# Silu activations and high-part splits of gated values held back until the next unit by seven has issued its copies out of PSUM

## The chip, the core and the metric

The kernel runs on one core of a Trainium2 chip. TensorE (PE) multiplies matrices and sums into PSUM; VectorE (DVE) and ScalarE (ACT) do elementwise work and read PSUM; GpSimd (POOL) helps in some stages; SyncE (SP) issues most DMAs. Each engine works through its own queue in a fixed order, and waits on semaphores for the others. The metric is the device time of one execution in microseconds: 1941.19 us before, the median of three runs between 1939.77 and 1942.38.

## What is computed

A decoder trunk of two layers over 512 tokens of width 1024, in float32. Each layer is: half a feed-forward block, a mixer (an mLSTM in the first layer, sparse attention in the second), half a feed-forward block. The change lies in the feed-forward block:

```python
def swiglu(h, w_in, w_out):
    a, b = jnp.split(h @ w_in, 2, axis=-1)
    return (jax.nn.silu(a) * b) @ w_out

h = h + 0.5 * swiglu(rmsnorm(h, ffn_norm[layer, 0]), ffn_w_in[layer, 0], ffn_w_out[layer, 0])
```

There are four such blocks, with 1024 inputs, 2 x 2816 columns of `w_in` (`a` and `b`) and 2816 rows of `w_out`.

## The kernel before

All of it stays on the core: eight tiles `h` of 128 features x 512 tokens hold the stream. The stages follow each other as `ffn0`, `mlstm`, `ffn1`, `kv`, `ffn2`, `nsa`, `ffn3`. To keep float32 accuracy every operand of a matmul is split in two: ScalarE copies it rounded into a high part (`whi`, `xhi`, `ghi`, L245 or L167), VectorE subtracts that from the value for the low part (`wlo`, `xlo`, `glo`, L246 or L170), and TensorE makes three products of parts (`mm3`, L236).

Columns of `w_in` are taken in blocks of 128, 22 for `a` and 22 for `b`. In the blocks 0, 1 and 3 (`SEVEN`) most pairs of blocks are multiplied as 2 x 2 block matrices by a scheme with seven products in place of eight: a **unit by seven** (`by_seven`, L473). Its seven products of 12 matmuls each go into three PSUM tiles A, Z, B of 512 columns, each half for itself: (1) A left, (2) Z right, (3) B left, (4) A right, (5) Z left, (6) Z right, (7) A left. Products 1, 5 and 6 take the normed input (`xhi`, `xlo`), products 2, 3, 4 and 7 sums of its quarters (`thi`, `tlo`). After each of the first four products ScalarE copies a half tile to SBUF (L481): `fw` after 1, `fu` after 2 and 3, `fw` after 4. Product 5 adds onto Z, where product 2 has been copied from, so it waits for the second copy. VectorE then adds Z (L497) and A (L502), and the unit returns two blocks of columns, `u1` and `u2`.

Gate blocks and value blocks alternate: a unit on two blocks of `a`, then a unit on the two blocks of `b` that go with them. After the gate unit `silu` (L403) multiplies by the norm's factor (L406, VectorE) and activates (L408, ScalarE). After the value unit `gate` (L411) multiplies both (L415, VectorE; L414 first in the last third) and splits the product into `ghi` and `glo`. The 22 pairs of blocks are taken in thirds of 8, 8 and 6 (`EVENS`); after each third the parts of its gated values are multiplied by the rows of `w_out` (the down product, weights `wraw`, splits at L167 and L170).

The weights of a unit are fetched as four quarters `q` (256 KB each), VectorE makes four sums of them (L197 to L200, `s`), and the seven forms are split in four groups, one unit ahead of TensorE. A scheduler below the program decides each engine's order within what the code's sequence and the data allow; `with tc.issue_after(ins)` holds instructions of the block behind `ins` on its own engine. The splits of the next unit's weights, the four copies, the activations and the `ghi` splits all share ScalarE's queue.

## Time and profile before

| what | value |
|---|---|
| median of three runs | 1941.19 us |
| profiled execution, its own time | 1940.4 us |
| its span, first to last instruction | 1938.6 us |
| granted TensorE clock, mean | 0.998 |
| PE / DVE / ACT busy | 99% / 81% / 53% of the span |
| copies of units (L481) | 57 units x 4 copies |
| activations behind units and strips (L408) | 66, 631 ns each |
| `ghi` splits (L245) | 88, 628 ns each |

[...] Matmuls of 256 columns last 0.28 us and start every 0.11 us. In the time line a bracket at the end of a row gives how long the engine sat idle before it and what ended that. A row of windows gives the stretch, its length, then busy time and count for each engine shown, the granted clock, the DMA share and GB/s.

### The profile page before, as it was taken

To read this page: it belongs to the slowest core of one execution; us is meant where nothing else is said; L and a number is where in the kernel's file an instruction comes from. 1 tells how busy PE (TensorE), PEld (TensorE's weight loads), DVE (VectorE), ACT (ScalarE), POOL (GpSimd) and SP (SyncE) were. 2 spreads that over 40 slices of the span, in tenths; PEclk is the share of its full clock that TensorE was granted. 3 is DMA by queue.
4 is the path that set the end of the run, shared out by engine and by line. 5 is a ranking of instruction groups with operands and counts; after the bars stand their busy time and mean duration, and the time that the engine had idled before them with its cause. 6 is when DMAs were issued, how large, how long until landed. Compare 5 with 4: busy or idle time off the path is not lost. (4 is left out here: it accounts for less than half of the span.)

```text
span 1938.6 us, 31636 instructions
## 1 busy us (share of the span) xinstructions
PE 1913.0 (99%) x11946; PEld 1693.3 (87%) x11946; DVE 1567.4 (81%) x2947; ACT 1024.9 (53%) x1979; POOL 168.1 (9%) x222
## 2 busy tenths in 40 slices
PE   9999999999999999999999999999999999999999
PEld 7989898788878999898888989898877788999897
DVE  8969788757889879697676979696899989879695
ACT  6536345445656446265354535354777766445262
POOL 0000001012200000001100000001444410000000
PEclk9999999999999999999999999999999999999999
DMA  5333322323132323323343332323322222323322
GB/s 192 115 98 104 120 83 71 116 82 96 66 126 82 122 86 104 103 72 116 117 129 107 115 113 101 103 66 113 107 66 55 66 100 86 120 88 105 101 74 93
DMA packets 81945, 192.80 MB, mean 99 GB/s; under 512 B 9920, under 2 KB 10944, under 8 KB 81792
## 3 DMA queue, kind: packets, MB, share of 16 engines
q1 hardware_dynamic: 80272, 187.76, 30.3%
q8 instruction: 94, 1.54, 0.3%
q0 software_dynamic: 512, 1.31, 0.3%
q10 hardware_dynamic: 1008, 1.70, 0.2%
q14 instruction: 59, 0.48, 0.1%
HBM read 177.10 MB, written 2.10 MB: 92 GB/s over the span
## 5 line engine op out<-in xcount | busy, mean ns | idle before, releaser
L236 PE MATMUL pmm<-xhi,whi 128*128 128x256 f32 (+1 forms) x1376 | 441.4, 321 | 6.7 <-ACT fu L481 6.1
L236 PE MATMUL pmm<-xhi,wlo 128*128 128x256 f32 (+1 forms) x1376 | 437.5, 318 | 0.4 <-DVE wlo L170 0.4
L236 PE MATMUL pmm<-xlo,whi 128*128 128x256 f32 (+1 forms) x1376 | 437.0, 318 | 0.8 <-DVE xlo L290 0.8
L167 ACT ACTIVATE whi<-wraw 128x512 fp32r<-128x512 f32 (+3 forms) x258 | 204.8, 810 | 269.6 <-PE pmm L236 163.2
L236 PE MATMUL pmm<-thi,whi 128*128 128x256 f32 x1184 | 328.8, 278 | 2.4 <-ACT fw L516 2.0
L236 PE MATMUL pmm<-thi,wlo 128*128 128x256 f32 x1184 | 327.5, 277 | 1.4 <-DVE wlo L246 1.4
L236 PE MATMUL pmm<-tlo,whi 128*128 128x256 f32 x1184 | 327.7, 277 | 0.0
L170 DVE TENSOR_TENSOR wlo<-wraw,whi 128x512 fp32r<-128x512 f32 (+3 forms) x258 | 240.3, 944 | 70.6 <-ACT whi L167 67.8
L236 PEld LDWEIGHTS pmm<-xhi,whi 128*128 128x128 f32 x1376 | 258.4, 188 | 26.2 <-ACT fu L481 7.7
L236 PEld LDWEIGHTS pmm<-xhi,wlo 128*128 128x128 f32 x1376 | 258.4, 188 | 20.1 <-DVE wlo L170 0.7
L236 PEld LDWEIGHTS pmm<-xlo,whi 128*128 128x128 f32 x1376 | 258.6, 188 | 19.8 <-DVE xlo L290 2.6
L245 ACT ACTIVATE whi<-q 128x512 fp32r<-128x512 f32 x260 | 163.9, 631 | 209.1 <-PE pmm L236 156.1
L236 PE MATMUL pmm<-glo,whi 128*128 128x512 f32 x704 | 274.4, 390 | 0.0
L236 PE MATMUL pmm<-ghi,whi 128*128 128x512 f32 x704 | 274.2, 389 | 0.0
L236 PE MATMUL pmm<-ghi,wlo 128*128 128x512 f32 x704 | 273.9, 389 | 0.0
L236 PEld LDWEIGHTS pmm<-thi,whi 128*128 128x128 f32 x1184 | 223.2, 189 | 4.0 <-ACT fw L516 3.3
L236 PEld LDWEIGHTS pmm<-thi,wlo 128*128 128x128 f32 x1184 | 223.0, 188 | 1.6 <-DVE wlo L246 1.6
L236 PEld LDWEIGHTS pmm<-tlo,whi 128*128 128x128 f32 x1184 | 223.4, 189 | 0.0
L246 DVE TENSOR_TENSOR wlo<-q,whi 128x512 fp32r<-128x512 f32 x260 | 178.0, 685 | 16.4 <-ACT whi L245 16.4
L245 ACT ACTIVATE whi<-s 128x512 fp32r<-128x512 f32 x222 | 138.5, 624 | 54.6 <-PE pmm L236 32.7
L236 PEld LDWEIGHTS pmm<-glo,whi 128*128 128x128 f32 x704 | 132.2, 188 | 28.0 <-DVE glo L246 1.1
L236 PEld LDWEIGHTS pmm<-ghi,wlo 128*128 128x128 f32 x704 | 132.2, 188 | 27.6
(380 smaller groups left out, 3246.7 us busy)
## 6 DMA issues: line engine op xcount, KB each, us to landing
q<-in_ffn_in SPq DMA_DIRECT2D x260, 256.0 KB, 2.6
wraw<-in_ffn_out SPq DMA_DIRECT2D x48, 512.0 KB, 3.5
wraw<-in_ffn_out SPq DMA_DIRECT2D x48, 384.0 KB, 3.1
wraw<-in_ffn_in SPq DMA_DIRECT2D x27, 512.0 KB, 3.8
e<-in_ffn_in SPq DMA_DIRECT2D x36, 256.0 KB, 2.7
wraw<-in_m_qk SPq DMA_DIRECT2D x8, 512.0 KB, 3.6
wraw<-in_m_v SPq DMA_DIRECT2D x8, 512.0 KB, 3.6
wraw<-in_m_og SPq DMA_DIRECT2D x8, 512.0 KB, 3.6
```

The lines of the kernel that those rows point to most:

```text
L167: t = nc.scalar.activation(hi[:p, c], raw[:p, c], AF.Copy)
L170: nc.vector.tensor_tensor(lo[:p, c], raw[:p, c], hi[:p, c].bitcast(F32), op=ALU.subtract)
L236: self.nc.tensor.matmul(out, lhsT, rhs, start=start, stop=stop, skip_group_check=shared)
L245: self.nc.scalar.activation(hi, src, AF.Copy)
L246: self.nc.vector.tensor_tensor(lo, src, hi.bitcast(F32), op=ALU.subtract)
```

## The change

Two closures are kept in a list `parked` in the three layers with units by seven: the activation of a gate value (L408; its multiplication at L406 is still issued at once), and the allocation and split of a gated value into `ghi` and `glo` (the multiplications are still issued at once). The next unit by seven issues what is kept directly after the copy of A right, the last of its four copies, and holds the ScalarE part of it behind that copy. At the end of each third, before the down product, what is still kept is issued. Gated values of the two plain blocks at a layer's start are not kept.

```diff
+            parked = deque()
+
+            def unpark():
+                while parked:
+                    parked.popleft()()
+
-            def silu(pa):
+            def silu(pa, park=False):
                 t = gp.tile([P, T], F32, name="ft", tag="ft", bufs=3 if seven else 2)
                 if seven:
                     TT(t, pa, r, op=ALU.mult)
                     pa = t
-                nc.scalar.activation(t, pa, AF.Silu)
+                if park:
+                    parked.append(lambda: nc.scalar.activation(t, t, AF.Silu))
+                else:
+                    nc.scalar.activation(t, pa, AF.Silu)
                 return t
...
                 TT(t, t, u, op=ALU.mult)
                 bufs = 8 if seven or not k0 else 6
-                hi = gp.tile([P, T], F32R, name="ghi", tag="ghi", bufs=bufs)
-                lo = gp.tile([P, T], F32R, name="glo", tag="glo", bufs=bufs)
-                self.split(t, hi, lo)
-                gs.append((hi, lo))
+
+                def parts():
+                    hi = gp.tile([P, T], F32R, name="ghi", tag="ghi", bufs=bufs)
+                    lo = gp.tile([P, T], F32R, name="glo", tag="glo", bufs=bufs)
+                    self.split(t, hi, lo)
+                    gs.append((hi, lo))
+
+                if park:
+                    parked.append(parts)
+                else:
+                    parts()
...
                 yield from product(A[:, l], s2, -2, False)
-                out(u1[:, r], A[:, l])
+                with tc.issue_after(out(u1[:, r], A[:, l]).ins):
+                    unpark()
...
-                            ts = [silu(t) for t in (yield from by_seven(p))]
+                            ts = [silu(t, seven) for t in (yield from by_seven(p))]
...
-                                ts.append(silu(pa))
+                                ts.append(silu(pa, seven))
                         for t, u in zip(ts, (yield from by_seven(FB + p))):
-                            gate(t, u)
+                            gate(t, u, seven)
...
+                unpark()
                 n = k1 - k0
                 for m in range(0, KB, 2):
```

The orders of TensorE, SyncE and GpSimd are the same before and after. Those of ScalarE and VectorE change in the three layers. The first place is ScalarE in the last layer, second third, in the gate unit with the blocks 14 and 15, where `ghi` belongs to the values of blocks 12 and 13. Before:

```order
L481 ACTIVATE fw_20059<-pmm_20056 128x256
L245 ACTIVATE ghi_20047<-ft_19908 128x512
L245 ACTIVATE whi_20106<-q11_19956 128x512
L245 ACTIVATE ghi_20052<-ft_19911 128x512
L481 ACTIVATE fu_20060<-pmm_20057 128x256
L245 ACTIVATE whi_20106<-s1_20091 128x512
L481 ACTIVATE fu_20060<-pmm_20058 128x256
L245 ACTIVATE whi_20138<-q22_19962 128x512
L481 ACTIVATE fw_20059<-pmm_20056 128x256
```

After (L497 is the copy's line there):

```order
L497 ACTIVATE fw_20051<-pmm_20048 128x256
L245 ACTIVATE whi_20098<-q11_19954 128x512
L497 ACTIVATE fu_20052<-pmm_20049 128x256
L245 ACTIVATE whi_20098<-s1_20083 128x512
L497 ACTIVATE fu_20052<-pmm_20050 128x256
L245 ACTIVATE whi_20138<-q22_19960 128x512
L497 ACTIVATE fw_20051<-pmm_20048 128x256
L245 ACTIVATE ghi_20130<-ft_19908 128x512
L245 ACTIVATE ghi_20134<-ft_19910 128x512
L245 ACTIVATE whi_20138<-s2_20084 128x512
```

The two `ghi` splits stood between the first and the second copy and now stand behind the fourth. The second place is VectorE in the same unit, from the gate's last multiplication on. Before:

```order
L415 TENSOR_TENSOR ft_19911<-ft_19911,fu_19918 128x512
L246 TENSOR_TENSOR wlo_20062<-q21_19822,whi_20061 128x512
L246 TENSOR_TENSOR glo_20048<-ft_19908,ghi_20047 128x512
L246 TENSOR_TENSOR glo_20053<-ft_19911,ghi_20052 128x512
L200 TENSOR_TENSOR s4_20093<-q12_19958,s2_20092 128x512
L246 TENSOR_TENSOR wlo_20107<-q11_19956,whi_20106 128x512
L246 TENSOR_TENSOR wlo_20107<-s1_20091,whi_20106 128x512
L246 TENSOR_TENSOR wlo_20139<-q22_19962,whi_20138 128x512
```

After (L424 is the multiplication's line):

```order
L424 TENSOR_TENSOR ft_19910<-ft_19910,fu_19916 128x512
L246 TENSOR_TENSOR wlo_20054<-q21_19814,whi_20053 128x512
L198 TENSOR_TENSOR s2_20084<-s1_20083,q11_19954 128x512
L246 TENSOR_TENSOR wlo_20099<-q11_19954,whi_20098 128x512
L200 TENSOR_TENSOR s4_20085<-q12_19956,s2_20084 128x512
L246 TENSOR_TENSOR wlo_20099<-s1_20083,whi_20098 128x512
L197 TENSOR_TENSOR s1_20227<-q21_20094,q22_20096 128x512
L246 TENSOR_TENSOR wlo_20139<-q22_19960,whi_20138 128x512
L199 TENSOR_TENSOR q21_20094<-q11_20090,q21_20094 128x512
L246 TENSOR_TENSOR glo_20131<-ft_19908,ghi_20130 128x512
L246 TENSOR_TENSOR glo_20135<-ft_19910,ghi_20134 128x512
```

The two `glo` subtractions came one operation behind the gate's multiplication and now come eight behind it; sums and low parts of the next units stand ahead of them. The third place is ScalarE in the value unit that ends this third. Before:

```order
L481 ACTIVATE fw_20197<-pmm_20194 128x256
L408 ACTIVATE ft_20188<-ft_20188 128x512
L408 ACTIVATE ft_20191<-ft_20191 128x512
L481 ACTIVATE fu_20198<-pmm_20195 128x256
L167 ACTIVATE whi_20238<-wraw_20236 128x1024
L481 ACTIVATE fu_20198<-pmm_20196 128x256
L481 ACTIVATE fw_20197<-pmm_20194 128x256
L167 ACTIVATE whi_20270<-wraw_20268 128x1024
```

After (L415 is the activation's line):

```order
L497 ACTIVATE fw_20195<-pmm_20192 128x256
L497 ACTIVATE fu_20196<-pmm_20193 128x256
L167 ACTIVATE whi_20236<-wraw_20234 128x1024
L497 ACTIVATE fu_20196<-pmm_20194 128x256
L497 ACTIVATE fw_20195<-pmm_20192 128x256
L415 ACTIVATE ft_20188<-ft_20188 128x512
L415 ACTIVATE ft_20190<-ft_20190 128x512
L167 ACTIVATE whi_20270<-wraw_20268 128x1024
```

The two activations moved from behind the first copy to behind the fourth, ahead of the split of the down product's second weight.

## The prediction

> **What bounds the kernel now.** I read the page first, then the list of waits, then the chain that ended last, and then the time line around the longest stall.

> ```profile
> span 1938.6 us, 31636 instructions
> PE 1913.0 (99%) x11946; PEld 1693.3 (87%) x11946; DVE 1567.4 (81%) x2947; ACT 1024.9 (53%) x1979; POOL 168.1 (9%) x222
> ```

> TensorE (PE) is busy for 1913.0 of 1938.6 us, so 25.6 us of idle time is nearly all that a change of order can win. The list of waits says who causes it (microseconds in total, times, longest):

> ```profile
> PE pmm L236 <- ACT fu L481: 6.1, 7, 2.0
> PE pmm L236 <- ACT fw L516: 2.0, 4, 0.7
> ```

> The first row is the largest single cause: seven times a matmul waits for a copy of a sum out of PSUM (`fu`, L481) on ScalarE (ACT). These copies belong to the units by seven. The second row is the other form of unit, which the change doesn't touch. The chain that ended last shows why such a copy is late:

> ```profile
> 1886.13 0.61 DVE ft L415
> ...
> 1886.77 0.97 ACT ghi L245 x2
> ...
> 1887.91 0.38 ACT fu L481
> ```

> VectorE (DVE) makes a gated value (L415), ScalarE waits for it to split off its high part (`ghi`), and the copy stands behind that split in ScalarE's queue. The longest stall, on ScalarE, VectorE and TensorE:

> ```profile
> 1779.11 0.38 ACT L481 ACTIVATE fw<-pmm 128x256 f32<-128x256 f32 x1 [0.79 <-PE pmm L236]
> 1783.16 0.63 ACT L245 ACTIVATE ghi<-ft 128x512 fp32r<-128x512 f32 x1 [3.66 <-DVE ft L415]
> 1783.69 0.61 ACT L245 ACTIVATE whi<-q 128x512 fp32r<-128x512 f32 x1
> 1784.21 0.61 ACT L245 ACTIVATE ghi<-ft 128x512 fp32r<-128x512 f32 x1
> 1784.73 0.36 ACT L481 ACTIVATE fu<-pmm 128x256 f32<-128x256 f32 x1
> 1783.04 0.68 DVE L415 TENSOR_TENSOR ft<-ft,fu 128x512 f32<-128x512 f32 x1
> 1782.88 0.28 PE L236 MATMUL pmm<-thi,wlo 128*128 128x256 f32 x1
> 1785.15 0.39 PE L236 MATMUL pmm<-xhi,whi 128*128 128x256 f32 x1 [1.99 <-ACT fu L481]
> ```

> ScalarE sat idle for 3.66 us before `ghi`, although the sum that `fu` copies had long been made: it is product two's, and products two to four are the 36 matmuls that end at 1782.88. Product five (the `xhi` at 1785.15) writes the same PSUM tile, so it waits for the copy.

> **The change, part by part.** *1. The stalls go.* The seven waits are priced from start to start, since a stalled matmul is followed by a slow restart that the idle time leaves out. Each window runs from the first matmul of product two to the first of product seven (36 + 24 matmuls). The first seven rows are the seven stalls; the next is an undisturbed unit.

> ```profile
> 74.62:82.06 7.44, 7.09 (x63) 1.00 0.28 88
> 195.36:203.60 8.24, 7.13 (x63) 1.00 0.25 87
> 297.67:305.24 7.57, 7.08 (x62) 1.00 0.00 0
> 760.22:768.42 8.20, 7.08 (x62) 1.00 0.24 87
> 862.42:870.01 7.59, 7.08 (x62) 1.00 0.01 2
> 1778.91:1789.17 10.26, 8.27 (x62) 0.88 0.32 105
> 1883.57:1891.17 7.60, 7.09 (x63) 1.00 0.01 2
> sum 56.90, PE 50.80; mean PE 7.26
> 1792.35:1799.15 6.80, 6.80 (x63) 1.00 0.40 130
> 1749.79:1756.89 7.10, 7.10 (x63) 1.00 0.35 111
> 1769.17:1776.19 7.02, 7.02 (x62) 1.00 0.28 96
> 1789.17:1790.99 1.82, 1.82 (x14) 0.76 0.38 137
> 1799.15:1800.51 1.36, 1.36 (x15) 1.00 0.44 121
> ```

> The seven take 56.90 - 7 x 6.80 = 9.30 us more than undisturbed ones. Two rows below show delays too short for the idle column, 0.30 and 0.22 us: 0.52. The last two rows are product seven after the longest stall and in an undisturbed unit: 0.46 more. Together 10.28 us.

> *2. A half-speed clock is part of this.* 10.26 stands out because the granted clock fell (the column after the counts):

> ```profile
> 1786.60:1790.00 3.40, 3.40 (x18) 3.40 (x17) 3.40 (x7) 1.35 (x4) 0.00 (x0) 0.50 0.45 149
> 1083.50:1086.90 3.40, 3.40 (x18) 3.40 (x17) 3.40 (x6) 1.26 (x2) 0.00 (x0) 0.50 0.53 170
> 1082.24 0.38 PE L236 MATMUL pmm<-thi,wlo 128*128 128x256 f32 x1 [1.37 <-DVE wlo L246]
> ```

> Both half-speed stretches begin 1.3 to 1.5 us after one of the two longest idle times (1.99 us until 1785.15, and 1.37 until 1082.24, in a layer that the change leaves alone). With a mean clock of 0.998 over 1938.6 us there is hardly room for a third. Stalls of 1.1 us (the windows from 195.36 and 760.22) show 1.00. So I charge this one to the stall: 3.40 us at half speed lose 1.70, which lies inside the 10.28. [...]

> *3. What is moved.* No instruction is added or removed. TensorE, SyncE and GpSimd keep their orders, so the DMAs are issued in the same sequence; no tile changes. The rows for the price and for the time that is left:

> ```profile
> 1792.83 1.27 ACT L408 ACTIVATE ft<-ft 128x512 f32<-128x512 f32 x2
> 1777.63 0.68 DVE L246 TENSOR_TENSOR wlo<-q,whi 128x512 fp32r<-128x512 f32 x1
> 1780.50 0.28 PE L236 MATMUL pmm<-thi,wlo 128*128 128x256 f32 x1
> 1797.99 1.23 DVE L170 TENSOR_TENSOR wlo<-wraw,whi 128x1024 fp32r<-128x1024 f32 x1 [1.41 <-ACT whi L167]
> 1801.67 0.39 PE L236 MATMUL pmm<-ghi,wlo 128*128 128x512 f32 x1
> 1796.63 0.38 ACT L481 ACTIVATE fw<-pmm 128x256 f32<-128x256 f32 x1 [0.97 <-PE pmm L236]
> ```

> On ScalarE two activations, or two `ghi` splits, move behind the fourth copy, 1.27 us for a pair (first row). Their results have time: an activation is wanted by L415, which needs product seven, and 24 + 12 more matmuls, some 4 us, lie between that and product four; the parts are read only in the down product, and what is kept at the end of a third is issued at once. What stands behind them now is the split of the next unit's weights, later by up to 1.27 us. It has more than that: the second and third rows are the low part of a weight and its first use, 1780.50 - 1778.31 = 2.19 us apart, in the run of units where VectorE lags most. If that cover were gone, the wait would come back as one for `wlo`.

> *4. What is late next.* VectorE, over two units (the columns are TensorE, weight load, VectorE, ScalarE, GpSimd):

> ```profile
> 1738.91:1758.25 19.34, 19.34 (x171) 19.15 (x169) 18.40 (x31) 12.65 (x26) 0.00 (x0) 1.00 0.32 101
> ```

> It is busy for 18.40 of 19.34 us, and an earlier TensorE doesn't make it faster. The critical place is the end of the same run: there 3.92 us of delay go (10.26 - 6.80 + 0.46), and the second `wlo` of the down product (1797.99 to 1799.22) has 2.45 us until its use at 1801.67. VectorE idled 1.41 us ahead of it, for a split behind a copy that itself waited for TensorE (last row of the fence before), so up to 1.41 us moves forward: 2.45 + 1.41 - 3.92 = -0.06. Nothing is left there, and the two activations that the new order puts ahead of that split can cost up to 1.27 us of the idle time that moved. The new wait lies between 0 (VectorE has its two `glo` splits later, so weights are earlier) and 1.5 us (2.45 - 3.92). I take 0.5, nearer to 0, since the idle time that moves is measured. At the other six stalls 0.6 to 1.4 us go, which a margin like this 2.45 covers.

> The sum: 10.28 - 0.5 = 9.8 us. The profiled execution took 1940.4 us, so 1930.6; the median of the runs, 1941.2, is 0.8 higher and would give 1931.4. I forecast **1931.0 us**.

> **The rivals.** *VectorE takes over and gives much back.* For it: the margin of -0.06 above, and a stall on ScalarE also gave VectorE time to catch up. Against: at the other six stalls less goes than the margin. If half of what goes came back as waits for `wlo` or `glo`, the gain is about 5 us: 1936.

> *The half-speed stretch isn't the stall's doing.* For it: its window may fall anywhere, and one cause in two cases is thin evidence. Against: no drop elsewhere at full work. The sum is 9.8 - 1.7 = 8.1: 1932.9. [...]

> *The parked work isn't really moved, or the copies stay late for another reason.* The recorded order has both splits directly behind the fourth copy, but the split of the next weights between the first and the second copy stays, and it waits for a buffer that TensorE frees. If that were the wait, 0 to 2 us would be won: 1940.

> *Slower.* `ghi` now waits, through the fourth copy, for TensorE's fourth product, and `glo` on VectorE waits for `ghi`; before, neither depended on that unit's matmuls. If VectorE reached `glo` first it would idle with the next weights queued behind. The price is 1 us in each of the 21 pairs that park splits (seven in each of three layers), less the 9.8 won: about 1952. It decides once `ghi` ends later than VectorE's eight operations behind L415, since that many now stand between. One of them takes 0.6 us:

> ```profile
> 1777.02 0.69 DVE L197 TENSOR_TENSOR s<-q,q 128x512 f32<-128x512 f32 x1 [1.38 <-issue]
> ```

> The next starts 0.61 us later, at 1777.63. Eight are 4.8 us; in the stall above L415 ended at 1783.72, so `glo` would come at 1788.5. The fourth product's last matmul starts at 1782.88, and one weight split, the copy and the two `ghi` behind it, 0.63 + 0.36 + 1.27, are done by 1785.5. In a unit where VectorE doesn't lag, L415 comes 3 us sooner and the two meet at the same time, so there is no wait to speak of.

> **How the numbers follow.** Forecast case (1929 to 1932.4): 0.60. Half-speed stretch stays: 0.12, 1932.9. VectorE takes over: 0.17, 1933 to 1938. Nothing moves: 0.08, 1940. Slower: 0.03, up to 1952. The range reaches from 1928.5 (all 10.28 won, the other half-speed stretch gone by chance as well) to 1937.0, which leaves out some 0.15. A measurement of this kernel tells about 0.2% from no change, 3.9 us, so faster means below 1937.3: the first two cases and nearly all of the third, 0.87; the same 0.10; slower 0.03.

> **What would show it.** In the profile after, the row "PE pmm L236 <- ACT fu L481" is gone or under 0.5 us; each of the seven places takes about 6.80 us from product two to seven; no half-speed stretch lies in the last layer's second third; the starts of `fu` no longer follow `ghi`. A new row of TensorE for `wlo` at L170 or L246 above 1.5 us would mean that VectorE took over. A wait of VectorE's `glo` for `ghi` above 1 us a pair would show the slower case. If the waits go but the time stays, the sum by start to start was wrong.

## The result, and the profile after

| | before | after |
|---|---|---|
| median of four runs each | 1941.51 us | 1930.40 us |
| range of the runs | 1939.77 to 1942.38 | 1929.94 to 1931.83 |
| profiled execution | 1940.4 | 1930.37 |
| its span | 1938.6 | 1928.5 |

The ratio is 0.9945, with a 95% interval of 0.9928 to 0.9962: faster by 0.55%. Profile against profile, 10.03 us are gone; the prediction's sum was 9.8. The head of the page of the changed kernel:

```profile
span 1928.5 us, 31657 instructions
PE 1908.6 (99%) x11946; PEld 1690.2 (88%) x11946; DVE 1564.4 (81%) x2947; ACT 1030.1 (53%) x1979; POOL 168.2 (9%) x222
```

TensorE idles for 19.9 us where it idled for 25.6. In its list of waits there is no row for `fu` any more; the other form of unit keeps its row:

```profile
PE pmm L236 <- ACT fw L533: 1.7, 4, 0.7
```

The seven places of the prediction, in the same form of windows (first matmul of product two to the first of product seven; the number behind the five counts is the granted clock), and last a later window of the same third:

```profile
75.41:82.21 6.80, 6.80 (x63) 6.80 (x62) 6.80 (x12) 4.66 (x10) 0.00 (x0) 1.00 0.26 85
195.13:201.93 6.80, 6.80 (x62) 6.80 (x61) 6.59 (x12) 4.66 (x10) 0.00 (x0) 1.00 0.38 126
295.82:302.62 6.80, 6.80 (x63) 6.80 (x61) 6.80 (x12) 4.66 (x10) 0.00 (x0) 1.00 0.00 0
757.52:764.32 6.80, 6.80 (x63) 6.80 (x61) 6.52 (x12) 4.66 (x10) 0.00 (x0) 1.00 0.34 116
858.20:865.00 6.80, 6.80 (x62) 6.80 (x61) 6.80 (x12) 4.66 (x10) 0.00 (x0) 1.00 0.00 1
1772.78:1779.58 6.80, 6.80 (x62) 6.80 (x61) 6.80 (x12) 4.66 (x10) 0.00 (x0) 1.00 0.33 102
1874.20:1881.00 6.80, 6.80 (x62) 6.80 (x61) 6.80 (x12) 4.66 (x10) 0.00 (x0) 1.00 0.01 2
...
1786.60:1790.00 3.40, 3.40 (x32) 3.40 (x31) 3.37 (x7) 2.58 (x4) 0.00 (x0) 1.00 0.31 98
```

All seven take 6.80 us at a granted clock of 1.00; the place of the longest stall, the sixth row, had 10.26 us at 0.88 before. The place of the longest stall in the time line, on ScalarE and VectorE:

```profile
1772.98 0.38 ACT L497 ACTIVATE fw<-pmm 128x256 f32<-128x256 f32 x1 [0.79 <-PE pmm L236]
1774.23 0.63 ACT L245 ACTIVATE whi<-q 128x512 fp32r<-128x512 f32 x1 [0.86 <-PE pmm L236]
1774.77 0.36 ACT L497 ACTIVATE fu<-pmm 128x256 f32<-128x256 f32 x1
...
1777.75 1.14 ACT L245 ACTIVATE ghi<-ft 128x512 fp32r<-128x512 f32 x2
...
1776.60 0.69 DVE L424 TENSOR_TENSOR ft<-ft,fu 128x512 f32<-128x512 f32 x1
```

The second copy comes 1.79 us after the first (1774.77 - 1772.98), where it came 5.62 us after it before (1784.73 - 1779.11). VectorE is hardly less late than it was: its second gated product starts 3.62 us after the first copy, and 3.93 before. But nothing that TensorE needs soon stands behind it now.

The new wait is where it was predicted, at the down product of that third, in TensorE's time line:

```profile
1790.46 0.40 PE L236 MATMUL pmm<-ghi,whi 128*128 128x512 f32 x1
1790.69 0.40 PE L236 MATMUL pmm<-glo,whi 128*128 128x512 f32 x1
1791.08 0.50 PE L236 MATMUL pmm<-ghi,wlo 128*128 128x512 f32 x1
1791.42 0.40 PE L236 MATMUL pmm<-ghi,whi 128*128 128x512 f32 x1
1791.66 0.40 PE L236 MATMUL pmm<-glo,whi 128*128 128x512 f32 x1
1792.22 0.50 PE L236 MATMUL pmm<-ghi,wlo 128*128 128x512 f32 x1 [0.16 <-DVE wlo L170]
```

The idle column shows 0.16 us, but the two matmuls on `wlo` start 0.39 and 0.56 us after the ones ahead of them, where 0.23 is usual (1790.46 to 1790.69): 0.49 us in all, against 0.5 in the sum.

### The profile page after: what moved, and what is told of

It reads as the page before. It is cut to its first block, busy times and chain, and to the rows that moved or that the text cites. A ratio compares the mean times of both kernels' runs of the same rounds, so it can differ in the third digit from the quotient of the medians.

```text
span 1928.5 us, 31657 instructions
## 1 busy us (share of the span) xinstructions
PE 1908.6 (99%) x11946; PEld 1690.2 (88%) x11946; DVE 1564.4 (81%) x2947; ACT 1030.1 (53%) x1979; POOL 168.2 (9%) x222
## 4 chain that ended last, share of the span: by engine, by line
PE 85%; DVE 9%; ACT 3%; issue 1%; DMA 1%; POOL 0%; SPq 0%; DVEq 0%; ACTq 0%
PE pmm L236 76%; PE vps L236 1%; PE S L236 1%; PE po L236 1%; DVE wlo L246 1%; PE pt L1288 1%; DVE wlo L170 1%; PE paux L236 1%; DVE pr L1253 1%; ACT pr L1256 1%; PE pn L236 1%; DVE ptl L246 1%; ACT whi L167 0%; PE pt L236 0%; PE dm L236 0%
## 5 line engine op out<-in xcount | busy, mean ns | idle before, releaser
L236 PE MATMUL pmm<-xhi,whi 128*128 128x256 f32 (+1 forms) x1376 | 439.2, 319 | 0.5 <-ACT whi L167 0.4
L236 PE MATMUL pmm<-xhi,wlo 128*128 128x256 f32 (+1 forms) x1376 | 436.7, 318 | 0.4 <-DVE wlo L170 0.4
L236 PE MATMUL pmm<-xlo,whi 128*128 128x256 f32 (+1 forms) x1376 | 436.1, 317 | 1.0 <-DVE xlo L290 0.8
L167 ACT ACTIVATE whi<-wraw 128x512 fp32r<-128x512 f32 (+3 forms) x258 | 204.8, 809 | 262.6 <-PE pmm L236 150.3
L236 PE MATMUL pmm<-thi,whi 128*128 128x256 f32 x1184 | 328.6, 278 | 2.3 <-ACT fw L533 1.7
L236 PE MATMUL pmm<-thi,wlo 128*128 128x256 f32 x1184 | 327.3, 277 | 1.4 <-DVE wlo L246 1.4
L236 PE MATMUL pmm<-tlo,whi 128*128 128x256 f32 x1184 | 327.3, 277 | 0.0
L170 DVE TENSOR_TENSOR wlo<-wraw,whi 128x512 fp32r<-128x512 f32 (+3 forms) x258 | 239.8, 943 | 73.8 <-ACT whi L167 71.6
L245 ACT ACTIVATE whi<-q 128x512 fp32r<-128x512 f32 x260 | 164.4, 632 | 233.9 <-PE pmm L236 204.5
L236 PEld LDWEIGHTS pmm<-xlo,whi 128*128 128x128 f32 x1376 | 258.0, 188 | 19.9 <-DVE xlo L290 2.6
L236 PEld LDWEIGHTS pmm<-xhi,wlo 128*128 128x128 f32 x1376 | 257.8, 187 | 20.0 <-DVE wlo L170 0.7
L236 PE MATMUL pmm<-glo,whi 128*128 128x512 f32 x704 | 274.5, 390 | 0.0
L236 PE MATMUL pmm<-ghi,wlo 128*128 128x512 f32 x704 | 274.2, 389 | 0.2 <-DVE wlo L170 0.2
L236 PE MATMUL pmm<-ghi,whi 128*128 128x512 f32 x704 | 274.2, 389 | 0.0
L236 PEld LDWEIGHTS pmm<-xhi,whi 128*128 128x128 f32 x1376 | 258.0, 187 | 18.0 <-ACT whi L167 0.8
L236 PEld LDWEIGHTS pmm<-thi,whi 128*128 128x128 f32 x1184 | 223.0, 188 | 3.8 <-ACT fw L533 2.9
L236 PEld LDWEIGHTS pmm<-thi,wlo 128*128 128x128 f32 x1184 | 222.8, 188 | 1.6 <-DVE wlo L246 1.6
L236 PEld LDWEIGHTS pmm<-tlo,whi 128*128 128x128 f32 x1184 | 222.9, 188 | 0.0
L246 DVE TENSOR_TENSOR wlo<-q,whi 128x512 fp32r<-128x512 f32 x260 | 177.6, 683 | 13.5 <-ACT whi L245 13.5
L245 ACT ACTIVATE whi<-s 128x512 fp32r<-128x512 f32 x222 | 138.0, 622 | 58.0 <-PE pmm L236 32.4
L236 PEld LDWEIGHTS pmm<-ghi,wlo 128*128 128x128 f32 x704 | 132.2, 188 | 28.4 <-DVE wlo L170 1.0
L236 PEld LDWEIGHTS pmm<-glo,whi 128*128 128x128 f32 x704 | 132.2, 188 | 28.3 <-DVE glo L246 1.4
```

Of the source, the lines that this page charges most:

```text
L167: t = nc.scalar.activation(hi[:p, c], raw[:p, c], AF.Copy)
L170: nc.vector.tensor_tensor(lo[:p, c], raw[:p, c], hi[:p, c].bitcast(F32), op=ALU.subtract)
L236: self.nc.tensor.matmul(out, lhsT, rhs, start=start, stop=stop, skip_group_check=shared)
L245: self.nc.scalar.activation(hi, src, AF.Copy)
L246: self.nc.vector.tensor_tensor(lo, src, hi.bitcast(F32), op=ALU.subtract)
```

## The experiments

A gate unit works on two blocks of `a`, a value unit on two of `b`. In a gate unit VectorE makes the gated products of the pair before (L424), and it is `ghi` that can stand ahead of the copies; in a value unit it multiplies the gate's values by the norm's factor (L412), and it is the activations that can. **VectorE's lag** below is the time from the start of a unit's first copy to the end of the second of these two operations. Each set of runs has its own runs of the kernel before (medians 1943.2, 1945.1 and 1943.0 us), so kernels are compared by their ratio to those. The changed kernel has runs in a set with a median of 1941.5 us for the kernel before, and none in these three sets. The kernels in the last three rows ran once each, so for them the time of that run is given. The waits are those of one profile of each kernel.

| run | ratio to before, 95% | waits for `fu`, us (times) |
|---|---|---|
| changed kernel | 0.9945 (0.9928 to 0.9962) | none |
| only the splits parked | 1.0007 (0.9997 to 1.0016) | 4.7 (9) |
| only the activations parked | 0.9941 (0.9928 to 0.9953) | 0.2 (1) |
| both, behind the second copy | 0.9933 (0.9920 to 0.9946) | none |
| both, behind the first copy | 1.0006 (0.9994 to 1.0018) | 6.8 (9) |
| one pair not parked | 0.9939 (0.9925 to 0.9953) | 1.0 (1) |
| before, three buffers for `q` | 0.9974 (0.9963 to 0.9985) | 2.7 (7) |
| only the splits, three buffers | 0.9963 (0.9950 to 0.9976) | 0.8 (3) |
| changed, third block's splits parked too | 0.9944 (0.9926 to 0.9962) | none |
| the same with three buffers | 0.9932 (0.9913 to 0.9952) | none |
| only the activations parked, more work for VectorE | one run, 1931.27 us | 0.2 (1) |
| changed, more work for VectorE | one run, 1931.40 us | none |
| changed, second copies repeated | one run, 1946.33 us | 0.4 (1) |

### Each half alone

```diff
 # only the splits
-ts = [silu(t, seven) for t in (yield from by_seven(p))]
+ts = [silu(t) for t in (yield from by_seven(p))]
...
-ts.append(silu(pa, seven))
+ts.append(silu(pa))
 # only the activations
-gate(t, u, seven)
+gate(t, u)
```

> Only the ghi/glo splits are parked; the gate activations go back to where they were before. Theory (the seven stalls are copies standing behind ghi): the row 'PE pmm L236 <- ACT fu' stays away and the time is 1931 +- 0.7 us, at most 1 us above the changed kernel's 1930.4, no half-speed stretch in the last layer. Rival (it is the activations that hold the copies up): most of the seven waits come back, about 1938 to 1940.

> Only the gate activations are parked; the ghi/glo splits are issued at once, as before. Theory (the stalls are copies standing behind ghi): all seven waits for ACT fu stay, about 6 us of idle time, the longest still near 2 us with a half-speed stretch behind it; the time is 1940 to 1941, within 1 us of before. Rival (activations): under 1933.

Both theories fell, and in opposite directions. The splits alone bring nothing that can be measured (1.0007); the activations alone bring as much as both (0.9941). With the splits alone parked, the longest stall lies in the value unit one ahead. From its time line, for ScalarE, VectorE and TensorE:

```profile
1772.12 0.38 ACT L497 ACTIVATE fw<-pmm 128x256 f32<-128x256 f32 x1 [0.79 <-PE pmm L236]
1775.89 1.29 ACT L417 ACTIVATE ft<-ft 128x512 f32<-128x512 f32 x2 [3.38 <-DVE ft L412]
1777.08 0.36 ACT L497 ACTIVATE fu<-pmm 128x256 f32<-128x256 f32 x1
...
1769.75 0.69 DVE L197 TENSOR_TENSOR s<-q,q 128x512 f32<-128x512 f32 x1 [1.00 <-DMA q<-in_ffn_in]
...
1770.96 1.28 DVE L246 TENSOR_TENSOR glo<-ft,ghi 128x512 fp32r<-128x512 f32 x2
...
1775.77 0.68 DVE L412 TENSOR_TENSOR ft<-fu,r 128x512 f32<-128x512 f32 x1
...
1777.50 0.39 PE L236 MATMUL pmm<-xhi,whi 128*128 128x256 f32 x1 [1.33 <-ACT fu L497]
```

The copy now stands behind two activations that wait for VectorE, exactly as it stood behind `ghi`. And VectorE has become later: its lag is 1776.45 - 1772.12 = 4.33 us here, where the corresponding value unit of before has 3.57 (1772.94 - 1769.37, from the rows below). The rows show a reason: L197, the first sum of the next quarters, idles 1.00 us for their DMA, and the two `glo` come behind it; in the time line of before they stand ahead of L197 in that unit (1763.11 and 1766.24), which hardly waits there. Over the whole kernel L197's waits for `q` (its DMA, or the `wlo` that lets it start) show it, in VectorE's list of waits (us in total, times, longest), first of before, then of the splits alone:

```profile
DVE s L197 <- DMA q<-in_ffn_in: 3.3, 6, 0.7
DVE s L197 <- DVE wlo L246: 3.1, 7, 0.5
DVE s L197 <- issue: 1.4, 1, 1.4
```

```profile
DVE s L197 <- DMA q<-in_ffn_in: 13.3, 18, 1.6
DVE s L197 <- DVE wlo L246: 2.3, 6, 0.5
```

That is 7.8 us before and 15.6 us with the splits alone (the changed kernel is between, 10.8 and 1.4). The splits alone also bring waits of TensorE that the kernel before doesn't have, at the last down product of each of the three layers:

```profile
PE pmm L236 <- ACT ghi L245: 1.5, 3, 0.6
PE pmm L236 <- DVE glo L246: 0.7, 3, 0.2
```

These 2.2 us are more than the 1.4 us by which the waits for `fu` fell. With the activations alone parked, the time line of the gate unit in which before has its longest stall reads:

```profile
1774.50 0.38 ACT L497 ACTIVATE fw<-pmm 128x256 f32<-128x256 f32 x1 [0.79 <-PE pmm L236]
1776.91 1.24 ACT L245 ACTIVATE ghi<-ft 128x512 fp32r<-128x512 f32 x2 [2.02 <-DVE ft L424]
1778.05 0.37 ACT L497 ACTIVATE fu<-pmm 128x256 f32<-128x256 f32 x1
...
1776.80 0.68 DVE L424 TENSOR_TENSOR ft<-ft,fu 128x512 f32<-128x512 f32 x1
```

The copy still stands behind both `ghi`, but VectorE's lag is only 2.98 us (4.61 before), and the copy comes 3.55 us after the first. By the stall of before, 5.62 us with 1.99 us of idle time, it is in time up to 3.63. So this half is in time at this place by only 0.08 us.

Why VectorE is later where the activations aren't parked shows only in part. The time line of before, one unit ahead of the longest stall, for ScalarE, VectorE and SyncE's queue:

```profile
1769.37 0.39 ACT L481 ACTIVATE fw<-pmm 128x256 f32<-128x256 f32 x1 [0.79 <-PE pmm L236]
...
1772.37 0.63 ACT L408 ACTIVATE ft<-ft 128x512 f32<-128x512 f32 x1 [2.62 <-DVE ft L406]
...
1773.18 0.62 ACT L408 ACTIVATE ft<-ft 128x512 f32<-128x512 f32 x1
1773.70 0.62 ACT L245 ACTIVATE whi<-q 128x512 fp32r<-128x512 f32 x1
...
1772.26 0.68 DVE L406 TENSOR_TENSOR ft<-fu,r 128x512 f32<-128x512 f32 x1
1772.86 0.68 DVE L246 TENSOR_TENSOR wlo<-q,whi 128x512 fp32r<-128x512 f32 x1
...
1774.35 0.69 DVE L246 TENSOR_TENSOR wlo<-q,whi 128x512 fp32r<-128x512 f32 x1 [0.21 <-ACT whi L245]
...
1773.57 0.33 SPq L188 DMA_DIRECT2D q<-in_ffn_in  x1
```

The activations wait for VectorE; the split of `q` stands behind them in ScalarE's queue; its low part on VectorE, at 1774.35, idles 0.21 us for the split. The longer idle time, 1.38 us ahead of L197 at 1777.02, doesn't come from that split. The last quarter that L197 reads has its DMA issued at 1773.57, right behind the low part at 1772.86 that read the old quarter last, and by the trace it landed at 1776.94, 3.37 us later. (The DMA that the later low part released, issued at 1775.07, landed at 1777.84, when L197 had started.) The low part at 1772.86 follows the two products with `r` without idle time, so it is VectorE's own lag that delays the transfer for which VectorE then waits.

From the first copy of the third's second unit to the end of the gated products, VectorE idles 2.6 us for L197 and 0.5 for splits of weights before, and 1.8 us and nothing with the activations parked. Over the whole kernel the waits of L197 for `q` are the same, 7.8 us in both. How the parked activations bring about the smaller lag isn't shown beyond that: the scheduler gives VectorE another order as well.

### The place of release

```diff
 # behind the second copy (for the other run: behind the first, out(u1[:, l], A[:, l]))
-out(u2[:, r], Z[:, r])
+with tc.issue_after(out(u2[:, r], Z[:, r]).ins):
+    unpark()
...
-with tc.issue_after(out(u1[:, r], A[:, l]).ins):
-    unpark()
+out(u1[:, r], A[:, l])
```

> The parked work is issued behind the second copy (the one product five waits for) instead of the fourth. Theory (only the second copy was ever late; copies three and four have slack until product seven, 24 matmuls and 2.7 us later): no wait for ACT fu or fw in the first, second or fourth feed-forward layer above 0.3 us, the time within 1 us of the changed kernel, 1929.5 to 1931.5. Rival (copies three and four are nearly as tight, so the place behind the fourth is needed): waits of product seven for ACT fw come back, 1 us or more each in several units, above 1933.

> The parked work is issued behind the first copy of the next unit, that is ahead of the second, the one product five waits for. Theory (what costs is that this copy stands behind work of ScalarE that waits for VectorE): the waits for ACT fu are back, 4 to 9 us in seven or more units, and the ratio to before is 0.997 to 1.003. Rival (parking itself helps, through another order on VectorE, wherever the work is released): no waits for fu, 0.993 to 0.996.

Both came as the theory says: 0.9933 behind the second copy and 1.0006 behind the first. The two programs differ in that one place. With the release behind the first copy the longest stall and the half-speed stretch behind it are back as before (1.99 us, 0.50). From its time line and its windows:

```profile
1791.25 0.39 PE L236 MATMUL pmm<-xhi,whi 128*128 128x256 f32 x1 [2.04 <-ACT fu L497]
```

```profile
1791.49:1794.90 3.41, 3.41 (x18) 3.41 (x18) 3.41 (x7) 1.81 (x5) 0.00 (x0) 0.50 0.41 145
```

So parking as such doesn't help; it matters whether the second copy is ahead of what waits for VectorE. VectorE's lag differs too between these two runs (3.35 us and 4.66 at this place), but the changed kernel, with a lag of 4.30 us there, has no wait: its copy depends on VectorE no longer. With the activations alone parked the copy does still depend on it, and VectorE is just early enough.

### One pair not parked

```diff
-gate(t, u, seven)
+gate(t, u, seven and (i, p) != (3, 12))
```

> The changed kernel, but one pair is not parked: the splits of blocks 12 and 13 in the last layer, which stood ahead of the copy in the longest stall. Theory (the half-speed stretch belongs to that stall): an idle time of 1.4 to 2 us comes back at that unit and a granted clock of 0.50 for 3.4 us follows, together 3.3 to 4.0 us more than the changed kernel, 1933.6 to 1934.4. Rival (the stretch has another cause): the stall comes back with the clock at 1.00 behind it, 1.6 to 2.3 us more, 1932.0 to 1932.7. Third case: VectorE comes to this place earlier now, so that the stall is under 1 us and the time under 1931.8; then nothing is said on the clock.

The third case: the stall is back with 0.96 us, and says nothing on the clock there. But in the same profile, in the third feed-forward block, which the edit leaves alone, stands a longer one in the time line:

```profile
1185.12 0.42 PE L236 MATMUL pmm<-thi,whi 128*128 128x256 f32 x1 [2.23 <-ACT fw L533]
```

The windows behind both stalls, this one and the one of 0.96 us (the column after the counts is the granted clock):

```profile
1185.33:1188.73 3.40, 3.40 (x17) 3.40 (x17) 3.35 (x7) 1.29 (x3) 0.00 (x0) 0.50 0.28 86
1784.00:1787.40 3.40, 3.40 (x31) 3.40 (x31) 3.40 (x6) 2.95 (x8) 0.00 (x0) 1.00 0.38 112
```

Behind 2.23 us the granted clock was 0.50 for the 3.40 us of the first row; behind 0.96 us it was 1.00.

### VectorE's lag and the buffers of q

```diff
-self.qbufs = 2 if seven else 1
+self.qbufs = 3 if seven else 1
```

> The kernel before, with nothing parked, but three buffers instead of two for each quarter of a weight (q) in the layers by seven. Theory after the first four runs (VectorE falls behind because it idles for the DMA of q, which starts only when the low part of an older q is done; the copy stalls since what stands ahead of it waits for that late VectorE): the waits of L197 for q go, VectorE's second gated product ends at most 3 us after the first copy of its unit (4.6 in the longest stall), the waits for ACT fu fall from 6.1 to under 1 us, the time is 1930 to 1933. Rival (VectorE is late because it has 18.4 us of work in 19.3, not because of q): the waits for ACT fu stay at 4 to 6 us, 1938 to 1941.

> Only the splits parked, with three buffers for each q. Theory (with the splits alone parked VectorE falls further behind, since its two low parts no longer lie in the time in which it waits for q, and the copy now stands behind the gate activations): with a third buffer the waits of L197 go, VectorE's lag falls as it did in q3_before, the waits for ACT fu fall from 4.7 to 1.5 to 3 us, ratio to before 0.996 to 0.998. Rival (VectorE's lag there isn't due to q): 4 to 5 us stay, 0.999 to 1.002.

In the kernel before, a third buffer takes every wait of L197 for `q` away, VectorE's lag at the longest stall falls from 4.61 to 3.02 us (the theory said at most 3), and no half-speed stretch is left before the kernel's end. (That one of the two is gone by chance is the author's estimate: the wait of 1.37 us ahead of it, in the third block, is still there, 1.38 us, and would be divided otherwise among the cells described under "Doses of idle time".) But the waits for `fu` fall only to 2.7 us, and the time to 0.9974, about half of the gain (theory and rival each said another number): in value units the copy still stands behind the activations, 4.20 us after the first one, 0.57 us too late. With the splits parked, where L197 waited most, the buffer does more than was expected: 4.7 us of waits become 0.8, and 1.0007 becomes 0.9963. So waits for `q` are one cause of VectorE's lag, 1.59 of 4.61 us at that place. They are only part of why the splits alone bring nothing: with three buffers in both, the splits' 0.9963 can't be told from 0.9974 without them.

### More work for VectorE

```diff
+for _ in range(times): TT(t, pa, r, op=ALU.mult)
-TT(t, pa, r, op=ALU.mult)
...
+ts = [silu(t, seven, 2 if (i, p) == (3, 10) else 1) for t in (yield from by_seven(p))]
```

> Only the gate activations parked, and VectorE is given two more operations (two products with r done twice, 1.2 us) once, in the second third of the last layer. Theory (this version has no stall only because VectorE's lag, 2.98 us in the third's last value unit, stays just under the 3.1 us or so at which the copy behind the two splits comes too late): the lag there is about 4.2 us, the copy comes 4.7 to 4.9 us after the first one (3.55 without), and a wait for ACT fu of 1.0 to 1.3 us is there. Rival (the copies were freed by something else): none above 0.3 us.

> The changed kernel with the same two operations more on VectorE. Theory (with both parked no copy depends on VectorE): every second copy in that third stays 1.36 to 1.8 us after the first, no wait for ACT fu; VectorE's lag at the end of the third goes from 5.5 to about 6.7 us, and the wait for the down product's wlo from 0.5 to 1 to 1.7 us. Rival: a wait for ACT fu there.

(What the first of these calls a value unit is, by the names used here, the gate unit of the longest stall.) Neither theory's larger lag came about: two more operations of 0.6 us each leave it at 3.11 us (2.98 without) with the activations parked, and at 5.47 us (5.46) at the end of the third in the changed kernel. With the activations parked the copy came after 3.69 us, and the wait was 0.06. The waits of L197 took the work up: in this third, up to the gated products of that unit, they fell from 1.8 to 0.8 us and from 3.3 to 2.0 us. The scheduler also put some of VectorE's operations in another order, so the two effects aren't apart. VectorE's lag didn't grow by the work that was added.

### Beyond the change

```diff
-gate(t, u, seven)
+gate(t, u, True)
...
-nc.scalar.activation(W[:, 0, :], X[:, :N], AF.Copy)
+with tc.issue_after(nc.scalar.activation(W[:, 0, :], X[:, :N], AF.Copy).ins):
+    unpark()
```

> The changed kernel, and the ghi/glo splits of the third feed-forward layer (units of the other form, one copy on ScalarE each) are parked too, until that copy. Theory (the four waits for ACT fw, 1.7 us, come from the copy standing behind ghi): the row is gone and the time is 1.7 to 3.0 us below the changed kernel, 1927.5 to 1929. Rival (as in the run with only the splits parked: the gate activations, which stay where they are there, become the late ones): the waits for ACT fw stay or other waits of the same size come, 1930 to 1932.

> The kernel of the run e7_apart with three buffers for each q in the layers by seven. Theory: VectorE's lag at the end of the second third of the last layer falls from 5.5 us to under 4, the wait for the down product's second wlo (0.5 us) goes, and the time is 0.3 to 1 us below e7_apart. Rival (that lag is VectorE's work): no difference.

The first theory fell in part. The row for `fw` isn't gone:

```profile
PE pmm L236 <- ACT fw L533: 2.7, 4, 2.0
```

But 2.0 of its 2.7 us are one stall, behind a transfer that landed late (last section); the other three waits make 0.7 us, against 1.7 in four in the changed kernel. The time, 0.9944, is like the changed kernel's, and the interval is too wide to tell the gain that was expected from none. In the long stall the copy itself waits for VectorE, with nothing ahead of it:

```profile
1184.03 0.38 ACT L533 ACTIVATE fw<-pmm 128x256 f32<-128x256 f32 x1 [3.71 <-DVE ft L424]
```

`fw` has one buffer in that block, and the gated product still reads it; the order in ScalarE's queue was not what bound it in this stall. With three buffers for `q` besides, the lag at the end of the last layer's second third is 3.37 us (5.46 in the changed kernel), and the wait for the down product's `wlo` is gone, as that theory says; the time, 0.9932, can't be told from 0.9944. No version here is measurably faster than the changed kernel.

### Doses of idle time

```diff
-out(u2[:, r], Z[:, r])
+for _ in range({(0, 4): 9, (0, 32): 13, (0, 40): 16, (1, 4): 10, (1, 32): 14,
+                (1, 40): 20, (3, 4): 11, (3, 32): 12, (3, 40): 15}.get((i, p), 1)):
+    out(u2[:, r], Z[:, r])
```

> The changed kernel with the second copy of nine chosen units repeated 9 to 20 times, so that product five waits. A copy takes about 0.27 us from start to start and there are 1.85 us of slack, so the idle times should be 0.3, 0.5, 0.8, 1.1, 1.3, 1.6, 1.9, 2.1 and 3.2 us (9, 10, 11, 12, 13, 14, 15, 16 and 20 copies). Theory (the clock is halved for 3.41 us after a window of 3.41 us in which TensorE idled for more than about half; the windows stand at multiples of 3.413 us from each other): half speed behind 16 and 20 copies unless a window's edge splits the idle time, perhaps behind 15, never behind 9 to 13. Rival (the stretch has nothing to do with the stall): half speed at none of the nine. [...]

This one missed its aim: the scheduler spread the repeated copies over the unit, between the other work of ScalarE, so that mostly the fourth copy came late and not the second (6.7 us of waits for it, ten times, at most 1.0 us), and no stall in those layers was over 1.05 us; none was followed by half speed. The windows could be tested on all profiles together, though. The records of the granted clock in the trace of before have 0.50 from 1083.487 and from 1786.633 us on, for 3.413 us each, and once more from 1940.232 on, at the kernel's end: 206 and 45 times 3.413 us lie between these starts. In the changed kernel the starts are 1077.395 (3.413 us long) and 1927.314, which is 249 times 3.413 us. So in each profile the start of a half-speed stretch was taken to fix a grid of 3.413 us, and TensorE's idle time in each cell of it was summed (without the last 20 us, where the kernel ends, and the first 5). In three profiles the only half-speed stretch is the one at the kernel's end, which then fixed the grid. Some of the profiles:

| profile | fullest cells, us of idle time | half speed behind it |
|---|---|---|
| one pair not parked | 2.23; 1.91 | yes; yes |
| release behind the first copy | 2.09; 2.04; 2.01 | yes, each |
| before | 1.93; 1.66 | yes; yes |
| only the splits parked | 1.76; 1.33 | yes; no |
| changed | 1.72; 1.03 | yes; no |
| only the splits, three buffers | 2.01; 1.63 | yes; no |
| only the activations parked | 1.57 | no |
| activations parked, more work | 1.53 | no |

In these 14 profiles the 17 cells with 1.66 us or more were followed by half speed, and no cell with 1.63 or less was.

## Why the prediction was right, and where it wasn't

The time, 1930.4 us, is 0.6 from the forecast. Term by term:

- **The stalls, 10.28 us.** Right. The seven windows are at 6.80 us each, and the longest, with its half-speed stretch and the restart, took its 3.92 us with it.
- **The half-speed stretch belongs to the stall.** Right, and now shown: the release behind the first copy brings back both (2.04 us, then 3.41 us at 0.50), and in the 14 profiles the granted clock fell behind the 17 cells with 1.66 us or more of idle time and behind no cell with 1.63 or less. The rival (1932.9) is out.
- **The new wait of 0.5 us** at the down product's second `wlo`. Right, 0.49, though it was a choice between bounds of 0 and 1.5 us, so the exact size is in part luck.
- **What is moved costs nothing.** The sum was right and a step was wrong. It put the whole gain on `ghi`, since the chain and the time line of before show `ghi` ahead of the late copies, and gave the activations a price of 0 and no gain. The total didn't show the mistake, because the change moves both. The runs show that moving `ghi` alone brings nothing, and moving the activations alone brings all of it. The chain showed what stood ahead of the copy; it didn't show why VectorE, for which it waited, was late, nor that the activations were next in line for the same wait.
- **VectorE "is busy for 18.40 of 19.34 us, and an earlier TensorE doesn't make it faster".** This took VectorE's lag for a matter of its work. A third buffer for `q` takes 1.59 us of the lag of 4.61 away, with no less work, and 1.2 us of added work added at most 0.13 us to it, though in another order of VectorE's operations.
- **VectorE takes over (1936).** It didn't. The lag did grow, to 5.46 us at the end of that third, but the only thing left behind it, the down product's `wlo`, cost 0.49 us.
- **Not moved (1940), and slower (1952).** Both out; the copies come 1.79 us after the first, and no wait of TensorE for `glo` or `ghi` appears. But two variants of the change, the splits alone and the release one copy sooner, did end at 1.0006 and 1.0007, so "nothing moves" was nearer than its 0.08 says.

Not settled is how the activations make VectorE late: how much of it comes through the weight splits behind them and how much through the other order that the scheduler then gives VectorE. No run has the one without the other.

## What to carry to other kernels

When a copy that the bounding engine needs stands behind an instruction that waits for a slower engine, moving that instruction away is worth little if the next one in the queue waits for the same engine (1.0007 here, with the splits alone): move all of them, or ask first why that engine is late. Measure each half of a change by itself; a correct total can hide that one half did nothing. The idle time just ahead of the lagging engine's operations (here the 1.38 us ahead of L197, for a transfer issued at 1773.57, when VectorE's own low part had ended at 1773.54) says more than its busy share.

## What the runs showed of the hardware that was not expected

A DMA of the same 256 KB landed late in the third feed-forward block in some profiles, also of kernels that leave this block as it was. From issue to the first sum that uses it, first in the time line of the changed kernel, then of the one with the third block's splits parked:

```profile
1170.58 0.33 SPq L188 DMA_DIRECT2D e<-in_ffn_in  x1
...
1173.42 0.69 DVE L197 TENSOR_TENSOR s<-e,e 128x512 f32<-128x512 f32 x1
```

```profile
1172.23 0.33 SPq L188 DMA_DIRECT2D e<-in_ffn_in  x1
...
1177.03 0.69 DVE L197 TENSOR_TENSOR s<-e,e 128x512 f32<-128x512 f32 x1 [2.10 <-DMA e<-in_ffn_in]
```

That is 2.84 and 4.80 us. By the landings in the traces this transfer took 4.4 to 4.9 us in seven of the 14 profiles and 2.5 to 3.1 in the others, those of before and after among them. The seven have the stall of 2.0 to 2.7 us of TensorE behind it, and six of them the half-speed stretch (with one pair not parked the 3.40 us at 0.50 from 1185.33 on), which costs 1.7 us more. What delays the transfer stayed open. So a single profile can differ from its kernel's median by more than several of the differences studied here: that of one pair not parked took 1936.56 us, and the median of its runs is 1931.59.
